# Down projection of a decoder layer on one Trainium2 core: 12 of 22 contraction blocks by a seven-product scheme

## The chip, the core and the metric

The kernel runs on one core of a Trainium2 chip. TensorE (PE, with its weight loads PEld), VectorE (DVE), ScalarE (ACT) and GpSimd (POOL) each work through a stream of instructions of their own, in order; SyncE (SP) issues most of the DMAs. The metric is the device time in microseconds of one execution, lower is better. Differences are judged on the median of several runs.

## The reference

One hybrid decoder layer is computed for 512 prompt tokens and 8 x 8 sample tokens, with model width 1024. Attention and a gated delta rule come first. The change concerns the end, the feed-forward part:

```
xn = rmsnorm(x, p['ln_ffn_pre'])
up, gate = jnp.split(xn @ p['w_ffn_in'], 2, axis=-1)
gate, new_ffn_conv = causal_dwconv(gate, ffn_conv_buf, p['ffn_conv_w'], p['ffn_conv_b'])
x = x + rmsnorm((jax.nn.gelu(gate) * up) @ p['w_down'], p['ln_ffn_post'])
```

`w_down` has 2816 rows (22 blocks of 128, the contraction) and 1024 columns (8 blocks of 128). 576 tokens go through it, 512 of the prompt and 64 samples. All of it is float32.

## The kernel before

**Products.** A float32 operand is split into a high part, a copy rounded to the type fp32r (ACT, line 314), and a low part, what the rounding lost (DVE, line 315). A product is three matmuls: high by high, high by low, low by high. The weight block of 128 x 128 is the stationary operand and the tokens stream as columns; the output stands transposed, 128 output features by tokens, in a bank of PSUM.

**Input projection.** `ffn_in` computes up and gate for each of the 22 blocks with a seven-product scheme already, on token halves of 290 columns, with weight sums on POOL. For block m, `times` (line 1895) multiplies gelu of the convolved gate by up into a buffer `gf`, once for each token half; `p7` and `p4` make the last two products of a block. `store` inside `ffn_in` transposes the conv's tails, four blocks at a time, for an output. At its end the splits of the first seven blocks begin (`divide_gf`, line 2051).

**Down projection.** `ffn_out` (line 2064) splits the other blocks: `ghi[k]` and `glo[k]` hold block k with 576 tokens. For each of 8 row blocks m of the output it takes two banks, one for tokens 256 to 575 (320 columns) and one for tokens 0 to 255, and goes through the 22 contraction blocks in chunks of 8, 8 and 6 (`chunks`). `weight` loads up to four blocks at a time (`wraw`, 256 KB) and splits them (`whi`, `wlo`). `product` makes 3 matmuls for each block. `store` (line 2098) copies the bank to `yT`, transposes it in pieces of 128 tokens, takes the sum of squares on ACT and multiplies by the norm's weight `lnfp` on DVE into `yn`. Row block 7 goes one half after the other, and `finish` (line 2129) makes the inverse roots, scales, adds the residual `x2` and stores the output.

**Order.** The program is written as straight Python loops; a list scheduler then orders each engine's stream by dependence and by the rotating buffers that a pool gives out for each name (`bufs`). `keep_in_program_order` pins single instructions. PSUM's banks have the names d (2), t (3), g (2), s (1) and m (1).

Of the kernel before, what the change touches and what calls it, by code (L numbers as in the profile page):

```python
# [9 lines left out]
F32 = mybir.dt.float32  # L10
F32R = mybir.dt.float32r
# [6 lines left out]
D = 1024  # L18
# [123 lines left out]
NC = 290  # L142
PLAIN = 3
# [7 lines left out]
class Body:  # L151
# [1618 lines left out]
    def ffn_in(self, firsts, sf, gx):  # L1770
# [6 lines left out]
        gfs = [  # L1777
            self.t(self.gtpool, [128, NQ], "gt", bufs=18) if m < 18 else None
            for m in range(NF)
        ]  # L1780
# [92 lines left out]
        def conv(st):  # L1873
# [4 lines left out]
            if i == 0:  # L1878
                self.tails = self.t(pool, [128, 18 * TAILS], "ftail", bufs=1)[:, : 18 * n]
# [15 lines left out]
        def times(eng, st, half, u):  # L1895
            if gfs[st["m"]] is None:
                gfs[st["m"]] = self.t(gx, [128, 2 * NC], f"gf{st['m']}")
            gf, y_ = gfs[st["m"]], st["y"]
            sl = slice(256 * half, 256 * half + 256)
            eng.tensor_tensor(out=gf[:, sl], in0=y_[:, sl], in1=u[:, 34:NC], op=ALU.mult)  # L1900
            eng.tensor_tensor(
                out=gf[:, 512 + 32 * half : 544 + 32 * half].rearrange("p (b t) -> p b t", b=4),
                in0=y_[:, 512:592].rearrange("p (b j) -> p b j", j=10)[:, 4 * half : 4 * half + 4, 2:10],
                in1=u[:, 0:32].rearrange("p (b t) -> p b t", b=4),
                op=ALU.mult,
            )
# [10 lines left out]
        def store():  # L1917

            if not waiting:
                return  # L1920
            m, n, tails = waiting.pop()
            tp = self.ps("s")
            self.transpose(tp[: 18 * n, :128], tails)
            rows = self.t(pool, [18 * TAILS, 128], "ftailT", bufs=1)
            nc.scalar.copy(rows[: 18 * n], tp[: 18 * n, :128])
            sl = slice(128 * m, 128 * (m + n))
            nc.gpsimd.dma_start(
                o["new_ffn_conv_prompt"][0, 0, :, sl].rearrange("r (m c) -> r m c", c=128), rows[0 : 2 * n]
            )
            nc.gpsimd.dma_start(  # L1930
                o["new_ffn_conv_sample"][0, :, :, sl].rearrange("b j (m c) -> (b j) m c", c=128), rows[2 * n : 18 * n]
            )
# [80 lines left out]
        for m in range(PLAIN, NF):  # L2013
# [22 lines left out]
            last = st  # L2036
        p7(last)
        self.gf, self.gx, self.ghi, self.glo, self.room = gfs, gx, [], [], []
        for p, j in (("hi", 1), ("lo", 1), ("hi", 2), ("lo", 2)):
            self.make_room(p, j)  # L2040
        for m in range(7):
            self.divide_gf(m)
        p4(last)
        store()

    def make_room(self, p, j):

        t = self.block_t(p, j).rearrange("p k c -> p (k c)")
        self.room += [t[:, 2 * NC * e : 2 * NC * e + SEQ + NS] for e in range(2)]

    def divide_gf(self, m, hi=None):

        hi = self.room.pop(0) if hi is None else hi
        if m == 0:
            lo = self.room.pop(0)
        elif m <= 18:
            lo = self.t(self.gtpool, [128, NQ], "gt", F32R, bufs=18)[:, : SEQ + NS]
        else:
            lo = self.t(self.gx, [128, 2 * NC], f"gf{m - 1}", F32R)[:, : SEQ + NS]
        self.split(hi, lo, self.gf[m][:, : SEQ + NS])  # L2060
        self.ghi.append(hi)
        self.glo.append(lo)

    def ffn_out(self, gh, pool, w3):
        nc, a, o = self.nc, self.a, self.o
        for m in range(7, 14):
            self.divide_gf(m, self.t(gh, [128, SEQ + NS], f"gh{m}", F32R))
        for p, j in (("hi", 3), ("lo", 3), ("hi", 4), ("lo", 4)):
            self.make_room(p, j)
        for m in range(14, NF):  # L2070
            self.divide_gf(m)
        ghi, glo = self.ghi, self.glo
        lnb = self.t(pool, [128, D], "lnfp")
        nc.scalar.dma_start(lnb, a["ln_ffn_post"][0].partition_broadcast(128))
        tiles = ((0, 128), (128, 128), (256, 128), (384, 128), (512, 64))
        groups = ((2, 5), (0, 2))
        yn = self.t(pool, [128, 5, D], "yn")
        ss = self.t(pool, [128, 5, 8], "yss")
        nc.vector.memset(ss, 1.0)
        junk = self.t(pool, [128, 128], "yjunk")  # L2080
        s1 = self.t(pool, [128, 5], "ys1")
        r = self.t(pool, [128, 5], "yr")
        roots = [self.t(pool, [128, 5], f"yroot{j}") for j in range(3)]
        nc.scalar.activation(roots[1], ss[:, :, 0], AF.Sqrt)
        x2s = []
        for i, (c0, n) in enumerate(tiles):
            x2 = self.t(pool, [128, D], "x2", bufs=5)
            nc.sync.dma_start(x2[:n], self.x2d[c0 : c0 + n])
            x2s.append(x2)

        def product(ps, w, k0, c):
            for k, (hi, lo) in enumerate(zip(*w), k0):
                gh, gl = ghi[k][:, c[0] : c[1]], glo[k][:, c[0] : c[1]]
                self.mm(ps, hi, gh, start=k == 0, stop=False)
                self.mm(ps, hi, gl, start=False, stop=False)
                self.mm(ps, lo, gh, start=False, stop=k == NF - 1)

        def store(ps, m, c, tl, late=None):
            yT = self.t(pool, [128, 320], "yT", bufs=3)
            nt = c[1] - c[0]  # L2100
            if m == 7 and tl[0] == 0:
                nc.vector.tensor_copy(yT[:, : nt // 2], ps[:, : nt // 2])
                nc.scalar.copy(yT[:, nt // 2 : nt], ps[:, nt // 2 :])
            else:
                nc.scalar.copy(yT[:, :nt], ps)
            ms = slice(128 * m, 128 * m + 128)
            if late is not None:
                for i in range(*tl):
                    t0 = tiles[i][0]
                    tp = self.ps("t")[:, :128]  # L2110
                    self.transpose(tp, yT[:, t0 - c[0] : t0 - c[0] + 128])
                    nc.scalar.activation(junk, tp, AF.Square, accum_out=ss[:, i, m : m + 1])
                    late.append((yn[:, i, ms], tp, lnb[:, ms]))
                return
            tp = self.ps4("t")
            for j, i in enumerate(range(*tl)):
                t0, n = tiles[i]
                self.transpose(tp[:n, j], yT[:, t0 - c[0] : t0 - c[0] + n])
            for j, i in enumerate(range(*tl)):
                n = tiles[i][1]  # L2120
                nc.scalar.activation(junk[:n], tp[:n, j], AF.Square, accum_out=ss[:n, i, m : m + 1])
            runs = ((0, 2, 128),) if tl[0] == 0 else ((0, 2, 128), (2, 1, 64))
            for j, nj, n in runs:
                nc.vector.tensor_tensor(
                    out=yn[:n, tl[0] + j : tl[0] + j + nj, ms], in0=tp[:n, j : j + nj],
                    in1=lnb[:n, ms].unsqueeze(1).to_broadcast([n, nj, 128]), op=ALU.mult,
                )

        def finish(tl, late):
            t = slice(*tl)  # L2130
            nc.vector.tensor_reduce(s1[:, t], ss[:, t], axis=AX.X, op=ALU.add)
            self.inverse_root(r[:, t], s1[:, t], 1.0 / D, EPS, [e[:, t] for e in roots])
            for out, tp, w in late:
                nc.vector.tensor_tensor(out=out, in0=tp, in1=w, op=ALU.mult)
            for i in range(*tl):
                c0, n = tiles[i]
                dst = o["y_prompt"][0, c0 : c0 + 128] if i < 4 else o["y_sample"].rearrange("b t d -> (b t) d")
                step = D if tl[0] else D // 2
                for d in range(0, D, step):
                    ds = slice(d, d + step)  # L2140
                    nc.vector.scalar_tensor_tensor(
                        out=yn[:n, i, ds], in0=yn[:n, i, ds], scalar=r[:n, i : i + 1], in1=x2s[i][:n, ds],
                        op0=ALU.mult, op1=ALU.add,
                    )
                    (nc.sync if (i + d // step) % 2 else nc.scalar).dma_start(dst[:, ds], yn[:n, i, ds])

        chunks = ((0, 8), (8, 8), (16, 6))
        ws = []
        for m in range(7):
            pp = [self.psd()[:, : c[1] - c[0]] for c in HALF_F]  # L2150
            for k0, nk in chunks:
                w = self.weight(a["w_down"][0], 128 * m, k0, nk)
                for p, c in zip(pp, HALF_F):
                    product(p, w, k0, c)
            if m > 3:
                ws.append(self.weight(a["w_down"][0], 128 * 7, *chunks[m - 4], pool=w3))
            for p, c, tl in zip(pp, HALF_F, groups):
                store(p, m, c, tl)
        for c, tl in zip(HALF_F, groups):
            p = self.psd()[:, : c[1] - c[0]]  # L2160
            for w, (k0, _) in zip(ws, chunks):
                product(p, w, k0, c)
            late = [] if tl[0] == 0 else None
            store(p, 7, c, tl, late)
            finish(tl, late or ())
# [43 lines left out]
```

## Time and profile before

| | |
|---|---|
| median of 3 runs | 1154.85 us (1153.15 to 1155.16) |
| profiled execution | 1153.75 us |
| its span | 1152.0 us, mean granted clock 0.996 |
| PE busy | 1115.3 us, 97% of the span |
| PEld, DVE, ACT, POOL busy | 1004.1, 717.3, 539.0, 220.5 us |
| first and last matmul of the down projection | 994.86 and 1142.60 us |

A row of the instructions by form names line, engine, operation, output and inputs, shapes, count, busy time with the mean of one, and the idle time ahead. A table of stretches gives for each stretch of the span the sum of busy time and, for engines other than the first, what they share with it. A chain lists start, duration, engine and line of the work that ended last. Line numbers belong to the kernel that the profile is of.

### The profile page before, as it was taken

The numbers are of one execution on the slowest core, as the hardware profiler recorded it, in microseconds if no ns is written. First come the engines' busy times: TensorE is split into PE (matmuls) and PEld (weight loads), VectorE is DVE, ScalarE is ACT, GpSimd is POOL, SyncE is SP. The second block draws the span as 40 slices with busy tenths as digits, with TensorE's granted clock in tenths as the row PEclk, the third lists the DMA queues.
The fourth block names the chain that finished last, engine by engine and source line by source line (L and its number), as shares of the span: only waits on it lengthen the run. The fifth ranks groups of instructions, "written<-read, shape, count | busy, mean of one in ns | idle before, by whom it ended". The sixth has DMA issues, their size and how long they took to land.

```text
span 1152.0 us, 23616 instructions
## 1 busy us (share of the span) xinstructions
PE 1115.3 (97%) x8683; PEld 1004.1 (87%) x8683; DVE 717.3 (62%) x1875; ACT 539.0 (47%) x1308; POOL 220.5 (19%) x342
## 2 busy tenths in 40 slices
PE   6999999999999999999999999999999999999997
PEld 5887887787787787789999977899999999999996
DVE  5456666695486377474343765499889889832323
ACT  5334445464464365352332344365565656732321
POOL 2022221020120010010000003333455444200000
PEclk9999999999999999999999999999999999999999
DMA  7366335737756956823232364323333332432322
GB/s 208 81 223 188 102 104 195 255 110 251 237 159 216 290 173 209 263 74 80 55 90 69 110 187 153 95 70 102 102 87 100 93 94 73 144 97 74 102 75 83
DMA packets 184347, 157.56 MB, mean 137 GB/s; under 512 B 12570, under 2 KB 146273, under 8 KB 184231
## 3 DMA queue, kind: packets, MB, share of 16 engines
q1 hardware_dynamic: 179713, 147.53, 42.0%
q0 software_dynamic: 3264, 5.16, 1.5%
q10 hardware_dynamic: 1254, 3.35, 1.0%
q8 instruction: 69, 1.13, 0.4%
q14 instruction: 47, 0.39, 0.1%
HBM read 146.12 MB, written 9.88 MB: 135 GB/s over the span
## 4 chain that ended last, share of the span: by engine, by line
PE 73%; issue 13%; DVE 6%; ACT 3%; POOL 3%; DMA 1%; SPq 0%; DVEq 0%; POOLq 0%; ACTq 0%
PE ps_d L272 26%; PE ps_t L272 18%; PE ps_g L272 15%; PE ps_s L272 7%; PE ps_t L420 7%; ACT KT L1399 1%; PE ps_m L272 1%; DVE cy L650 1%; DMA lk<-in_da_lambda_k 1%; POOL grr L384 1%; POOL gf L384 0%; DVE wlo L315 0%; DMA page<-in_cache_v 0%; POOL hss L384 0%; DVE row L970 0%
## 5 line engine op out<-in xcount | busy, mean ns | idle before, releaser
L272 PE MATMUL ps_d<-xhi,whi 128*128 128x256 f32 (+2 forms) x704 | 217.8, 310 | 0.2 <-DVE qm L1128 0.2
L315 DVE TENSOR_TENSOR wlo<-wraw,whi 128x512 fp32r<-128x512 f32 x196 | 137.9, 720 | 122.4 <-ACT whi L314 121.6
L272 PE MATMUL ps_d<-xhi,wlo 128*128 128x256 f32 (+2 forms) x704 | 213.3, 303 | 0.7 <-DVE wlo L315 0.7
L272 PE MATMUL ps_d<-xlo,whi 128*128 128x256 f32 (+2 forms) x704 | 212.8, 303 | 0.3 <-DVE xlo L315 0.2
L314 ACT CAST whi<-wraw 128x512 fp32r<-128x512 f32 (+1 forms) x198 | 117.3, 612 | 179.1 <-PE ps_d L272 93.8
L272 PEld LDWEIGHTS ps_d<-xhi,whi 128*128 128x128 f32 x704 | 133.6, 190 | 5.8 <-issue 4.2
L272 PEld LDWEIGHTS ps_d<-xlo,whi 128*128 128x128 f32 x704 | 133.9, 190 | 3.3 <-issue 2.4
L272 PEld LDWEIGHTS ps_d<-xhi,wlo 128*128 128x128 f32 x704 | 133.6, 190 | 2.5 <-issue 1.0
L1399 ACT COPY KT<-ps_t 128x512 f32<-128x512 f32 x106 | 57.2, 603 | 31.3 <-PE ps_t L420 30.8
L420 PE MATMUL ps_t<-consts,page 128*128 128x128 f32 x512 | 67.8, 279 | 0.3
L272 PE MATMUL ps_t<-fhit,hw 128*128 128x290 f32 x228 | 68.0, 298 | 0.0
L272 PE MATMUL ps_t<-flot,hw 128*128 128x290 f32 x228 | 67.7, 297 | 0.0
L272 PE MATMUL ps_t<-fhit,lw 128*128 128x290 f32 x228 | 67.6, 297 | 0.0
L420 PEld LDWEIGHTS ps_t<-consts,page 128*128 128x128 f32 x512 | 55.6, 140 | 13.8 <-issue 6.7
L314 ACT CAST hw<-sw 128x512 fp32r<-128x512 f32 x76 | 47.2, 622 | 41.4 <-PE ps_g L272 19.9
L315 DVE TENSOR_TENSOR lw<-sw,hw 128x512 fp32r<-128x512 f32 x76 | 60.1, 790 | 6.7 <-ACT hw L314 6.6
L272 PEld LDWEIGHTS ps_t<-flot,hw 128*128 128x128 f32 x228 | 43.2, 190 | 0.0
L272 PEld LDWEIGHTS ps_t<-fhit,lw 128*128 128x128 f32 x228 | 43.1, 189 | 0.0
L272 PEld LDWEIGHTS ps_t<-fhit,hw 128*128 128x128 f32 x228 | 43.0, 189 | 0.0
L1887 DVE SCALAR_TENSOR_TENSOR fy<-fpre,fw,fy 128x592 f32<-128x592 f32 x44 | 36.5, 830 | 2.5 <-ACT fy L1885 1.8
L272 PE MATMUL ps_s<-page,pT 128*32 128x256 f32 x512 | 35.3, 385 | 1.8 <-DMA page<-in_cache_v 1.6
L272 PE MATMUL ps_s<-KT,qb 128*32 128x256 f32 x512 | 35.7, 385 | 0.6
(688 smaller groups left out, 2990.1 us busy)
## 6 DMA issues: line engine op xcount, KB each, us to landing
page<-in_cache_k SPq DMA_DIRECT2D x128, 256.0 KB, 4.2
page<-in_cache_v SPq DMA_DIRECT2D x128, 256.0 KB, 4.4
wraw<-in_w_in SPq DMA_DIRECT2D x88, 256.0 KB, 3.0
wraw<-in_w_ffn_in SPq DMA_DIRECT2D x50, 256.0 KB, 3.0
wraw<-in_w_down SPq DMA_DIRECT2D x40, 256.0 KB, 3.2
raw<-in_w_ffn_in SPq DMA_DIRECT2D x38, 256.0 KB, 2.9
wraw<-in_w_out SPq DMA_DIRECT2D x16, 256.0 KB, 2.9
x<-in_x_prompt SPq DMA_DIRECT2D x4, 512.0 KB, 8.7
```

The lines of the kernel that those rows point to most:

```text
L272: return self.nc.tensor.matmul(out, lhsT, rhs, **kw).ins
L314: self.nc.scalar.copy(hi, raw)
L315: (eng or self.nc.vector).tensor_tensor(out=lo, in0=raw, in1=hi.bitcast(F32), op=ALU.subtract)
L384: nc.gpsimd.tensor_tensor(out=dst, in0=dst, in1=self.mhalf[:rows, :n], op=ALU.pow)
L420: self.nc.tensor.transpose(out, in_, self.ident[:k, :k])
L650: nc.vector.scalar_tensor_tensor(out=y, in0=pre[:, j : j + n], scalar=self.cw[:, ch, 24 + j : 25 + j], in1=y, op0=ALU.mult, op1=ALU.add)
L1399: copy(kt[:, :, 128 * j : 128 * j + 128], tp)
L1887: nc.vector.scalar_tensor_tensor(out=y, in0=pre[:, j : j + 592], scalar=fw[:, m, 16 + j : 17 + j], in1=y, op0=ALU.mult, op1=ALU.add)
```

## The change

Blocks 0 to 11 of the contraction are taken as 6 pairs (j, j + 6), the 8 row blocks as 4 pairs (2p, 2p + 1), and the 576 tokens as two halves of 288 (256 prompt tokens and 32 samples each). On each such 2 x 2 arrangement the eight block products are replaced by seven, of sums of weight blocks and of token blocks. Blocks 12 to 21 (`FLAT`: 6 and 4) stay plain, in the same halves of 288.

Pass one makes, for all four p, the three products that use unsummed token blocks (`"11"`, `"21"`, `"22"`), in two steps of three pairs (`stage_s`), and keeps sums in `saves`; `stage_l` adds the plain blocks of the upper row block there, ahead of them for p of 0 and 1 and after them for 2 and 3. Pass two takes p in turn: the plain blocks of the lower row block (`stage_f`), then t1 and t2 (`stage_t`), then t3 and t4 (`stage_e`). Weight loads of the seven products fetch three blocks with 256 columns (384 KB, `dx`, six buffers, two for each step). The token sums of t1 to t4 are made late in pass one by `sums_seven`, on ACT, DVE and POOL. Each of the 30 or so stages loads two stages ahead and prepares one ahead. The tail of the kernel scales on ACT and adds on POOL for one tile and a half, and the rest goes as before.

```
+NH = 288
+JS = 6
+STEPS = ((0, 3), (3, 3))
+FLAT = ((12, 6), (18, 4))
...
+        self.leads = self.weight(a["w_down"][0], 0, *FLAT[0])
         p7(last)
...
+        for m in range(2 * JS, 18):
+            self.divide_flat(m)
         p4(last)
-        store()
+        self.last_tail = store
...
+    def divide_seven(self, j, gh):
...
+        self.split(ab[:, 0:2], ab[:, 2:4], x)
+        self.split(c[:, 0], c[:, 1], y[:, 1])
+        g.tensor_tensor(out=y[:, 0], in0=y[:, 0], in1=x[:, 1], op=ALU.subtract)
+        g.tensor_tensor(out=y[:, 1], in0=y[:, 1], in1=y[:, 0], op=ALU.subtract)
...
+    def sums_seven(self, j):
...
+        self.pinned_split(c, lo, y)
+        t2 = y[:, 1].unsqueeze(1).to_broadcast([128, 2, NH])
+        self.nc.gpsimd.tensor_tensor(out=y, in0=t2, in1=ab[:, 0:2].bitcast(F32), op=ALU.subtract)
+        yield
+        self.tc.keep_in_program_order(
+            self.nc.vector.tensor_tensor(out=y, in0=y, in1=ab[:, 2:4].bitcast(F32), op=ALU.subtract)
+        )
+        yield
+        self.pinned_split(ab[:, 0:2], ab[:, 2:4], y)
...
+        def both(p, k0, nk):
+            t = self.t(w7, [128, 768], "dx", bufs=6).rearrange("p (k c) -> p k c", k=3)
+            nc.sync.dma_start(t, w[128 * k0 : 128 * (k0 + nk), 256 * p : 256 * p + 256].rearrange("(k p) c -> p k c", p=128))
+            return t[:, :, 0:128], t[:, :, 128:256]
...
+        def stage_s(p, i, banks):
...
+            def load():
+                x, y = both(p, k0, nk), both(p, JS + k0, nk)
+                op(nc.gpsimd, x[1], x[1], y[1], ALU.add)
+                return *x, y[0]
+
+            def prepare(raws):
+                a11, a21, a12 = raws
+                op(nc.vector, a21, a11, a21)
+                ws = [pair(a11), pair(a12)]
+                op(nc.vector, a21, a12, a21, ALU.add)
+                return [*ws, pair(a21)]
+
+            def run(ws):
+                b1, b2, b3 = banks()
+                product(b1, ws[0], "11", start=first, stop=end, **kw)
+                product(b2, ws[1], "21", start=first and p > 1, stop=end and p < 2, **kw)
+                product(b3, ws[2], "22", start=first and p > 1, stop=end and p < 2, **kw)
...
+        def finish(h, late=()):
...
+            nc.vector.tensor_copy(r4[32 * h : 32 * h + 32], r[last, 3 * h + 2 : 3 * h + 3])
...
+                    if i == 3 or i == 4 and d == 0:
+                        nc.scalar.activation(
+                            yn[rows, i, ds], yn[rows, i, ds], AF.Identity, scale=r[:, i + h : i + h + 1] if i < 4 else r4
+                        )
+                        op(nc.gpsimd, yn[rows, i, ds], yn[rows, i, ds], x2s[i, d][rows], ALU.add)
+                        nc.sync.dma_start(dst[:, ds], yn[rows, i, ds])
+                        continue
...
+        for i in range(len(stages) + 2):
+            if i < len(stages):
+                loaded.append(stages[i][0]())
+            if 0 < i <= len(stages):
+                ready.append(stages[i - 1][1](loaded.pop(0)))
+            if i > 1:
+                at[0] = i - 2
+                stages[i - 2][2](ready.pop(0))
```

The instructions of DVE move at three places (on PE, fourteen matmuls of 288 columns of the first plain stage stand ahead of the last up product where seven of 320 stood). On DVE, at the end of the splits, ahead of the first weights that follow the first plain stage (`wlo_13440` now; `gt`, `fhit`, `flot`, `ghab` name low parts of token blocks). Before:

```order
L315 TENSOR_TENSOR gt_13339<-gt_9910,flot_2491_13327 128x576
L315 TENSOR_TENSOR gt_13342<-gf_2396_12830,fhit_2492_13328 128x576
L315 TENSOR_TENSOR wlo_13501<-wraw_13496,whi_13500 128x512
L315 TENSOR_TENSOR gf_2499_13345<-gf_2426_12985,fhit_2492_13328 128x576
L315 TENSOR_TENSOR wlo_13504<-wraw_13498,whi_13500 128x256
L315 TENSOR_TENSOR gf_2500_13348<-gf_2455_13139,flot_2493_13329 128x576
L315 TENSOR_TENSOR gf_2501_13351<-gf_2463_13239,flot_2493_13329 128x576
```

and now:

```order
L319 TENSOR_TENSOR gt_13336<-gt_9908,gt_13336 128x288
L319 TENSOR_TENSOR gt_13344<-gt_9909,gt_13344 128x288
L319 TENSOR_TENSOR ghab_2493_13351<-gt_9904,ghab_2493_13351 128x576
L319 TENSOR_TENSOR gt_13352<-gt_9910,gt_13352 128x288
L2151 MEMSET yss_13368 128x48
L319 TENSOR_TENSOR wlo_13440<-wraw_13383,whi_13439 128x512
L319 TENSOR_TENSOR gf_2496_13360<-gf_2468_13250,gt_13359 128x576
L2190 TENSOR_TENSOR dx_13482<-dx_13482 128x3x128
L319 TENSOR_TENSOR lw_13522<-dx_13482,hw_13521 128x384
```

Of the splits of token blocks the last of the seven-product ones are 576 and 288 columns in turn, the next low weight part comes behind them, and the first subtraction of weight blocks (`dx`) behind that.

On DVE in the middle of the projection: `wlo` is a low part of plain weights, `yn` the output that is weighted by `lnfp`, `dx` raw weights of a step of `stage_s` or their sums, `lw` low parts of them, `yT` an output on its way to a transpose. Before:

```order
L2124 TENSOR_TENSOR yn_13356<-ps_t_14103,lnfp_13354 128x2x128
L2124 TENSOR_TENSOR yn_13356<-ps_t_14103,lnfp_13354 64x128
L2124 TENSOR_TENSOR yn_13356<-ps_t_14114,lnfp_13354 128x2x128
L315 TENSOR_TENSOR wlo_14292<-wraw_14287,whi_14291 128x512
L315 TENSOR_TENSOR wlo_14245<-wraw_14240,whi_14244 128x512
L315 TENSOR_TENSOR wlo_14248<-wraw_14242,whi_14244 128x256
```

and now, where steps of `stage_s` follow each other in pass one:

```order
L2190 TENSOR_TENSOR dx_13704<-dx_13704 128x3x128
L2190 TENSOR_TENSOR dx_13704<-dx_13706,dx_13704 128x3x128
L2190 TENSOR_TENSOR yT_13702<-ps_d_13393,consts_13377 128x288
L319 TENSOR_TENSOR lw_13711<-dx_13654,hw_13710 128x384
L319 TENSOR_TENSOR lw_13715<-dx_13656,hw_13714 128x384
L319 TENSOR_TENSOR lw_13720<-dx_13654,hw_13719 128x384
L2190 TENSOR_TENSOR dx_13754<-dx_13754 128x3x128
L2190 TENSOR_TENSOR dx_13754<-dx_13756,dx_13754 128x3x128
L2190 TENSOR_TENSOR yT_13752<-ps_g_13444,consts_13377 128x288
L319 TENSOR_TENSOR lw_13761<-dx_13704,hw_13760 128x384
L319 TENSOR_TENSOR lw_13765<-dx_13706,hw_13764 128x384
```


The two sums of a step's weights stand ahead of the low parts of the step before it; before, low parts of weights stood there with nothing but the products by `lnfp`.

On DVE at the end of the kernel, before:

```order
L2102 COPY yT_14870<-ps_d_14803 128x128
L2134 TENSOR_TENSOR yn_13356<-ps_t_14873,lnfp_13354 128x128
L2131 TENSOR_REDUCE ys_2506_13360<-yss_13357 128x2
L2134 TENSOR_TENSOR yn_13356<-ps_t_14876,lnfp_13354 128x128
L394 TENSOR_SCALAR yroot_2508_13362<-ys_2506_13360 128x2
L396 TENSOR_SCALAR yroot_2510_13364<-ys_2506_13360 128x2
L397 RECIPROCAL yr_13361<-yroot_2509_13363 128x2
L398 TENSOR_TENSOR yroot_2509_13363<-yr_13361 128x2
L399 TENSOR_TENSOR yroot_2509_13363<-yroot_2509_13363,yroot_2510_13364 128x2
L400 SCALAR_TENSOR_TENSOR yr_13361<-yroot_2509_13363,yr_13361 128x2
L2141 SCALAR_TENSOR_TENSOR yn_13356<-yn_13356,yr_13361,x_2511_13366 128x512 x2
L2141 SCALAR_TENSOR_TENSOR yn_13356<-yn_13356,yr_13361,x_2512_13368 128x512 x2
```

and now:

```order
L2190 TENSOR_TENSOR yT_15132<-ps_d_14885,fw_13363 128x288
L2245 TENSOR_REDUCE ys_2501_13370<-yss_13368 128x3
L2249 TENSOR_TENSOR yn_13367<-ps_t_15134,lnfp_13365 128x2x128
L398 TENSOR_SCALAR yroot_2504_13373<-ys_2501_13370 128x3
L400 TENSOR_SCALAR yroot_2506_13375<-ys_2501_13370 128x3
L2249 TENSOR_TENSOR yn_13367<-ps_t_15134,lnfp_13365 32x128
L401 RECIPROCAL yr_13371<-yroot_2505_13374 128x3
L402 TENSOR_TENSOR yroot_2505_13374<-yr_13371 128x3
L403 TENSOR_TENSOR yroot_2505_13374<-yroot_2505_13374,yroot_2506_13375 128x3
L404 SCALAR_TENSOR_TENSOR yr_13371<-yroot_2505_13374,yr_13371 128x3
L2247 COPY yr_2503_13372<-yr_13371 32x1
L2262 SCALAR_TENSOR_TENSOR yn_13367<-yn_13367,yr_13371,dx_15004 128x512
```

The eviction is an addition of 288 columns, a product by `lnfp` and a copy of a scale stand between the sum of squares and the scalings, and five scalings of 512 columns follow (the first shown) where four stood.

## What the change will do: the prediction

> **What bounds the kernel now.** I read the page's busy times first, then the table of stretches over the last 200 us, the chain that ended last, and the instructions by form. The busy times name the candidate, and the stretches show that it holds in the stage that the change rewrites.
>
> ```profile
> PE 1115.3 (97%) x8683; PEld 1004.1 (87%) x8683; DVE 717.3 (62%) x1875; ACT 539.0 (47%) x1308; POOL 220.5 (19%) x342
> 950.00:1000.00 50.00, 50.00 (x371) 49.94 (x371) 45.01 (x82) 34.77 (x65) 19.87 (x32) 1.00 0.31 94
> 1000.00:1050.00 50.00, 50.00 (x381) 49.66 (x380) 20.74 (x35) 18.21 (x50) 0.57 (x1) 1.00 0.38 110
> 1050.00:1100.00 50.00, 49.21 (x372) 48.58 (x372) 15.16 (x29) 17.14 (x55) 0.00 (x0) 1.00 0.33 94
> 1100.00:1143.00 43.00, 42.87 (x324) 42.16 (x322) 12.07 (x27) 10.80 (x40) 0.00 (x0) 1.00 0.15 48
> ```
>
> The columns are PE, PEld, DVE, ACT and POOL, then clock and DMA. From about 1000 us on, the down projection keeps PE busy without a gap at full clock, while DVE and ACT need a third of the time and POOL nothing. A matmul saved there is worth its cadence as long as the others can take on more work. Matmul records overlap, so I take cadences from the chain, where runs of equal matmuls stand end to end.
>
> ```profile
> 994.86 0.54 PE L272 MATMUL ps_t<-fhit,whi 128*128 128x320 f32 x2
> 988.49 3.23 PE ps_t L272 x24
> 1003.06 3.52 PE ps_t L272 x24
> 1006.58 2.84 PE ps_d L272 x24
> 1071.18 16.62 PE ps_d L272 x126
> 1089.37 16.62 PE ps_g L272 x126
> 1142.60 0.28 PE L272 MATMUL ps_d<-flot,wlo 128*128 128x256 f32 x1
> ```
>
> 24 matmuls of 290 columns take 3.23 us (134.6 ns each), of 320 columns 3.52 (146.7), of 256 columns 2.84 (118.3). Cost follows columns. One row block of the output is 66 of each width, 17.5 us; the two 126-rows start 18.19 apart, so five transposes take 0.7 us, 0.14 each.
>
> **Matmuls.** Before: 8 row blocks x 22 contraction blocks x 3 = 528 at each width: 528 x 146.7 + 528 x 118.3 = 139.9 us. After: 10 plain blocks give 8 x 10 x 3 x 2 = 480, and the seven products of 6 block pairs and 4 output pairs give 4 x 6 x 7 x 3 = 504: 984 of 288 columns. Between the 256 and 320 rows 288 comes to 132.5 ns; a 290 that is not reduced at all would be 134.6. I take 133, nearer the first since columns set the cost: 130.9 us. **Gain 9.0**, bounds 9.5 and 7.5.
>
> **Transposes.** A store now transposes 288 tokens in three full pieces, 16 stores x 3 = 48 against 40. Ahead of the last matmul stand 45 against 38: 7 x 0.14 = **+1.0**.
>
> **Waits of PE that go.** From 994.86 to 1142.72 PE spends 147.9 us: 139.9 of down matmuls, 1.6 of twelve late up matmuls, 39 transposes at 0.14 (5.6, the conv tails' one among them). **0.7** is left as waiting; it goes with the code that caused it.
>
> **The hand-over.** These rows price the splits and the queue of DVE.
>
> ```profile
> 999.27 0.41 DVE L1900 TENSOR_TENSOR gf<-fy,ps_t 128x256 f32<-128x256 f32 x1
> 999.70 3.94 DVE L315 TENSOR_TENSOR gt<-gt,gh 128x576 fp32r<-128x576 f32 x5
> L315 DVE TENSOR_TENSOR gt<-gt,gh 128x576 fp32r<-128x576 f32 x7 | 5.3, 758 | 0.1
> L315 DVE TENSOR_TENSOR lw<-sw,hw 128x512 fp32r<-128x512 f32 x76 | 60.1, 790 | 6.7 <-ACT hw L314 6.6
> L315 DVE TENSOR_TENSOR wlo<-wraw,whi 128x256 fp32r<-128x256 f32 x8 | 3.4, 420 | 0.9 <-ACT whi L314 0.9
> L315 DVE TENSOR_TENSOR wlo<-wraw,whi x34: 418/692/694, 1011.0 to 1098.2; 128x512 fp32r<-128x512 f32 x29, 128x256 fp32r<-128x256 f32 x5
> ```
>
> PE starts on blocks 12 to 17, ready early, with 14 matmuls ahead of the last up product where seven stood, so that product ends about 0.9 us later, covered. Behind it come 22 + 36 matmuls, 7.7 us from 998.4: PE wants the next weights' low part at 1006.2. On DVE that part stands behind seven splits of 576 and five of 288 from about 999.5: at 0.67 to 0.79 each for the long ones (0.758 less overlap, or the five in 3.94) and 0.4 for the short ones 6.9 to 7.7 us, and its own 0.6. It comes at 1006.9 to 1007.8, **+0.7** (0.6 to 1.6). No earlier: POOL's second differences wait for those splits, behind them POOL's first weight sum. The six first 384 KB loads start when the last up product frees their space, 1.0 us for issue, and have until 1012.6, PE's start S on the seven-product blocks.
>
> **Pass one is the doubtful place.** A stage there is 27 matmuls, 3.6 us. DVE does five 384-wide operations for it, 0.56 each by the straight line from the 0.42 and 0.69 rows: 2.8 us; ACT three copies; POOL one addition. Each fits. What need not fit is a ring: six load buffers hold three stages, and DVE runs in order.
>
> ```profile
> L1805 POOL TENSOR_TENSOR sw<-raw,raw 128x512 f32<-128x512 f32 x19 | 24.9, 1312 | 25.7 <-DVE lw L315 24.5 <-DMA raw<-in_w_ffn_in 1.2
> wraw<-in_w_down SPq DMA_DIRECT2D x40, 256.0 KB, 3.2
> page<-in_cache_k SPq DMA_DIRECT2D x128, 256.0 KB, 4.2
> x<-in_x_prompt SPq DMA_DIRECT2D x4, 512.0 KB, 8.7
> L310 SPq DMA_DIRECT2D wraw<-in_w_down x34: 367/368/460, 1011.7 to 1098.9; - x34
> L1910 DVE TENSOR_TENSOR p<-ps_t,p 128x290 f32<-128x290 f32 x19 | 8.6, 454 | 0.0
> ```
>
> The third low part of stage n frees its buffers; SP issues both loads for stage n+3 (2 x 0.37), they land (3.9, between the 3.2 of a quiet queue and the 4.2 of a full one), POOL adds (1.0, three quarters of 1.3), DVE forms two sums (1.1) and evicts a bank (0.45), and only then comes the first low part of stage n+2 (0.5): 8.0 us with 0.3 for semaphores, 9.0 with the other two low parts, for two stages, in which PE spends 7.2. The lead at the start pays for most of it. Stage 2's third low part stands at S + 2.3 (its buffer is released at S + 1.2, and DVE has three plain weights ahead of it). By the same ring stage 4 gets its first at S + 10.6, wanted at 11.0; stage 6 at S + 19.6, wanted at 18.2. The other chain, stages 3, 5, 7 (S + 6.5, 14.5, 23.5), just meets PE. **+1.5**, from 0 (landing in 3.2) to 5 (landing in 5). Plain weight loads stand in SP's queue between these; each can delay them by 0.37 and is counted once.
>
> GPSIMD Engine Reference, section of the specifications, in the Trainium skill, says that GpSimd and VectorE share SBUF interfaces and contend when a VectorE operation has two SBUF inputs, which speaks against adding GpSimd work here. The rows agree as far as they go: 790 ns for a 512-wide split in the stage where POOL works, 692 in the one where it idles. By that ratio a stage's DVE work is 3.2 us and the ring 0.2 longer: PE still bounds, and it would add about 0.3 to the sum.
>
> After pass one come 120 plain matmuls, 16 us, under which six blocks are summed and split anew (18 DVE operations of 576, 12 to 14 us, beside 5 of weights): full, but the second half is wanted only 10 us later. In pass two PE needs 17.6 us for each output pair and DVE some 11.5, so I add nothing; without that cover a wait is 0.5 us in each of four pairs.
>
> **The tail.**
>
> ```profile
> 1142.92 0.29 DVE L2102 COPY yT<-ps_d 128x128 f32<-128x128 f32 x1 [0.17 <-PE ps_d L272]
> 1143.69 0.28 ACT L2112 ACTIVATE yjunk<-ps_t 128x128 f32<-128x128 f32 x1
> 1144.11 0.28 ACT L2112 ACTIVATE yjunk<-ps_t 128x128 f32<-128x128 f32 x1
> 1144.51 0.17 DVE L2131 TENSOR_REDUCE ys<-yss 128x2 f32<-128x16 f32 x1
> 1146.01 2.74 DVE L2141 SCALAR_TENSOR_TENSOR yn<-yn,yr,x 128x512 f32<-128x512 f32 x4
> L2124 DVE TENSOR_TENSOR yn<-ps_t,lnfp 128x256 f32<-128x256 f32 x15 | 6.2, 414 | 20.1 <-ACT yjunk L2121 20.1
> wraw<-in_w_down SPq DMA_DIRECT2D x8, 128.0 KB, 2.2
> ```
>
> From the last matmul's start to the end 9.4 us pass. Now the eviction is one 288-wide sum (0.45 for 0.29: +0.15), DVE may still be at the other half's scaling (+0.3), there are three squares (+0.45), a 256-wide product stands between the sum of squares and the root (+0.35), a copy of a scale (+0.15), and a fifth scaling (+0.7): **+2.1**. If the last store, 128 KB, lands a microsecond sooner than one of 256 KB, +1.1; if nothing overlaps, +3.
>
> **Sum.** -9.0 + 1.0 - 0.7 + 0.7 + 1.5 + 2.1 = -4.4 us. The profiled execution took 1153.75 us (span 1152.0 and 1.75 around it), 1.1 below the median of the runs: it becomes 1149.4, and the median of 1154.85 becomes **1150.4**. With every bound good but the loads' 3.2: -9.5 + 1.0 - 0.7 + 0.6 + 0 + 1.1 = -7.5. What a measurement here can tell from no change is 0.2%, 2.3 us.
>
> **Rivals.** *Full cover* (chance 0.13): the loads land in 3.2 us and the last store early: -7.5, 1147.4. For it: wraw's row, DMA engines busy 0.31 to 0.38. Against it: two 384 KB loads go out together.
>
> *The ring eats the gain* (0.18): loads land in about 5 us, stages 4, 6 and 8 each come 2 us later than the last, waits of 5 to 6: 1154 to 1155. For it: the page loads' 4.2 with less in flight per load; the 0.7 of the hand-over may be 1.6 as well.
>
> *Slower* (0.27): the same ring with landings near the 8.7 of the first x loads, as when lnfp, x2, plain weights and six loads are in flight together. The ring is then 13.8 us for two stages, 6.9 for one against 3.6; over the five stages that use a second-hand buffer 16 us, less 2 of lead: +14 instead of +1.5, 1163. It turns the sign where waits pass 6.6 us, a landing of about 5.4. Against it: only four loads in the trace are so slow, at the start of the program.
>
> TensorE: Matmul & The Clock Gate, Part 1, in the Trainium skill, says that an idle window of some 3.4 us halves the matmul clock until a busy one has passed; the trace has 1.00 in every stretch of the projection and no wait that long there. By it a stall of 3.5 us or more would cost about another 1.7 us; single waits of the ring are 1.4 to 2, so the sum and the forecast hold without it.
>
> *It does not do what it says*: not possible for the count, since the matmuls are written out; 984 is fixed.
>
> **Chances.** Forecast 0.42 (own range 1148 to 1152.4), full cover 0.13: faster 0.55. The ring eating the gain 0.18: same. Slower 0.27. The range reaches from 1146.5, below full cover, to 1160, which takes in the lower half of the slower case; some 0.17 is left out.
>
> **What would show it.** Right: 984 matmuls of 288 columns at 132 to 134 ns; PE gaps, 1 to 2 us each, ahead of the first product of the sixth stage of pass one and ahead of the third plain stage; the tail 11 to 12 us. Wrong: a cadence above 135; gaps in every stage of pass one; gaps in pass two; loads that land in over 5 us.

## The result, and the profile after

The changed kernel takes 1175.33 us (median of 6 runs, 1173.78 to 1176.98) where the kernel before takes 1154.00 (1151.23 to 1155.79): ratio 1.0181, 95% interval 1.0167 to 1.0195. The forecast was 1150.4, so it lies 25 us off and on the wrong side.

The page of the changed kernel and its table of stretches (PE, PEld, DVE, ACT, POOL, clock, DMA), to set beside those of before:

```profile
PE 1113.3 (95%) x8619; PEld 1000.2 (85%) x8619; DVE 795.0 (68%) x1981; ACT 557.8 (48%) x1363; POOL 289.7 (25%) x396
1000.00:1050.00 50.00, 45.44 (x323) 44.11 (x322) 42.23 (x71) 27.94 (x61) 24.13 (x22) 0.97 0.67 204
1050.00:1100.00 50.00, 43.73 (x308) 42.85 (x307) 36.28 (x51) 18.23 (x44) 19.15 (x14) 0.93 0.28 84
1100.00:1150.00 50.00, 46.50 (x351) 45.59 (x351) 32.15 (x66) 25.61 (x86) 15.20 (x13) 1.00 0.21 67
1150.00:1173.00 23.00, 8.05 (x61) 7.58 (x59) 12.61 (x33) 6.20 (x23) 4.67 (x3) 0.75 0.29 103
```

PE, almost without a gap before, now loses 3.5 to 6.3 us in each 50, the clock falls below 1, and DVE, a third busy before, is busy for 64 to 84%. PE's waits from 760 us on (us in total, times, longest) say where:

```profile
PE ps_t L2229 <- DVE yT L2190: 5.4, 5, 2.2
PE ps_g L276 <- ACT whi L318: 4.0, 1, 4.0
PE ps_d L276 <- DVE wlo L319: 3.0, 1, 3.0
PE ps_t L2229 <- DVE yn L2241: 2.9, 2, 1.5
PE ps_t L276 <- ACT u L1850: 2.5, 1, 2.5
PE ps_g L276 <- DVE wlo L319: 1.1, 1, 1.1
```

Nearly all of it is DVE that comes late (ACT's `whi` too: its cast stood in ACT's stream behind a token sum that DVE had not made). The wait of 3.0 us is the hand-over, the passage from the input projection to the down projection. DVE and POOL there, in order of time (start, duration):

```profile
1005.43 0.74 DVE L319 TENSOR_TENSOR fhit<-gt,fhit 128x576 fp32r<-128x576 f32 x1
1006.10 1.36 DVE L319 TENSOR_TENSOR flot<-gt,flot 128x576 fp32r<-128x576 f32 x1
1007.39 0.45 DVE L319 TENSOR_TENSOR gt<-gt,gt 128x288 fp32r<-128x288 f32 x1
1007.76 0.75 DVE L319 TENSOR_TENSOR ghab<-gt,ghab 128x576 fp32r<-128x576 f32 x1
1008.42 2.25 DVE L319 TENSOR_TENSOR gt<-gt,gt 128x288 fp32r<-128x288 f32 x2
1010.60 1.34 DVE L319 TENSOR_TENSOR ghab<-gt,ghab 128x576 fp32r<-128x576 f32 x1
1012.89 0.63 DVE L319 TENSOR_TENSOR wlo<-wraw,whi 128x512 fp32r<-128x512 f32 x1
...
1005.59 1.26 POOL L2084 TENSOR_TENSOR gt<-gt 128x288 f32<-128x288 f32 x1 [1.73 <-DVE gt L319]
1007.92 1.25 POOL L2084 TENSOR_TENSOR gt<-gt 128x288 f32<-128x288 f32 x1
1009.25 1.12 POOL L2190 TENSOR_TENSOR dx<-dx,dx 128x384 f32<-128x384 f32 x1
1010.32 2.27 POOL L2084 TENSOR_TENSOR gt<-gt 128x288 f32<-128x288 f32 x2
```

The same subtraction of 576 columns takes 0.74 and 0.75 us where it starts just ahead of a subtraction on POOL, and 1.36 and 1.34 where one of POOL's is already running; two of 288 take 2.25 where 0.9 would do. DVE's operations with an input in PSUM do not show this: 288-wide additions from a bank are at 0.44 to 0.46 everywhere, beside POOL or not.

The tail, DVE first, then the SP queue and POOL:

```profile
1157.35 1.77 DVE L2262 SCALAR_TENSOR_TENSOR yn<-yn,yr,gt 128x512 f32<-128x512 f32 x1
1159.15 0.46 DVE L2190 TENSOR_TENSOR yT<-ps_d,fw 128x288 f32<-128x288 f32 x1
...
1163.58 3.75 DVE L2262 SCALAR_TENSOR_TENSOR yn<-yn,yr,dx 128x512 f32<-128x512 f32 x4
1167.25 0.73 DVE L2262 SCALAR_TENSOR_TENSOR yn<-yn,yr,x 64x512 f32<-64x512 f32 x1
...
1166.14 0.50 SPq L2260 DMA_DIRECT2D out_y_sample<-yn  x1
1166.74 1.02 SPq L2266 DMA_DIRECT2D out_y_prompt<-yn  x2
...
1164.38 1.73 POOL L2190 TENSOR_TENSOR yn<-yn,x 64x512 f32<-64x512 f32 x1 [4.14 <-ACT yn L2256]
```

The last product's eviction (`yT`) stands behind a scaling that took 1.77 us beside POOL's addition; four scalings take 3.75 us where 2.74 stood before; and in SP's queue two stores of finished rows stand behind the sample's, which waits for POOL.

Three marks of each profiled execution show where a kernel's time lies: the first matmul of the down projection, its last one, and the end.

| kernel | first | last | projection, last minus first | tail, end minus last | median, us |
|---|---|---|---|---|---|
| before | 994.86 | 1142.60 | 147.7 | 9.4 | 1154.00 |
| changed | 998.74 | 1157.21 | 158.5 | 16.0 | 1175.33 |
| all sums on DVE (e1) | 993.49 | 1135.16 | 141.7 | 16.0 | 1154.21 |
| weight and late token sums on DVE (e2) | 1001.22 | 1143.54 | 142.3 | 16.0 | 1159.25 |
| token differences on DVE (e3) | 996.78 | 1155.49 | 158.7 | 16.0 | 1173.14 |
| tail order alone (e4) | 996.51 | 1154.20 | 157.7 | 15.1 | 1174.18 |
| e1 with the tail reordered (e6) | 992.00 | 1133.32 | 141.3 | 12.3 | 1150.55 |
| e6 with early weights (e7) | 997.08 | 1137.76 | 140.7 | 12.2 | 1151.22 |
| e1 with idle additions on POOL (e8) | 998.49 | 1167.21 | 168.7 | 16.4 | 1182.45 |

The first mark also moves between executions, with the attention stages far ahead of the change: it stands at 994.86 in the kernel before and at 999.06 in the same kernel with idle work on POOL (e5, below), whose edit comes behind it. The projection (147.7 and 147.9) and the tail (9.4 and 9.5) do not move there.

Between the first two marks PE waits 14.3 us in the changed kernel and 3.6 with all sums on DVE. In the changed kernel the clock is also at half for some 10 us behind two of these waits (3.4 at the hand-over; 0.54 on average from 1065.5 to 1072.6). That is 10.7 and, by estimate, 5 of the 16.8 us between the two projections.

### The profile page after: what moved, and what is told of

The parts are those of the page before. It is cut to its first block, busy times and chain, and to the rows that moved or that the text cites. A ratio compares the mean times of both kernels' runs of the same rounds, so it can differ in the third digit from the quotient of the medians.

```text
span 1173.2 us, 23848 instructions
## 1 busy us (share of the span) xinstructions
PE 1113.3 (95%) x8619; PEld 1000.2 (85%) x8619; DVE 795.0 (68%) x1981; ACT 557.8 (48%) x1363; POOL 289.7 (25%) x396
## 4 chain that ended last, share of the span: by engine, by line
PE 64%; issue 15%; DVE 9%; POOL 4%; ACT 4%; DMA 3%; SPq 0%; DVEq 0%; POOLq 0%; ACTq 0%
PE ps_d L276 23%; PE ps_g L276 13%; PE ps_t L276 13%; PE ps_t L424 7%; PE ps_s L276 6%; ACT KT L1403 1%; POOL dx L2190 1%; DVE lw L319 1%; PE ps_m L276 1%; DMA dz<-in_w_down 1%; DMA dx<-in_w_down 1%; DVE wlo L319 1%; POOL grr L388 1%; DVE gt L319 1%; DVE yn L2262 1%
## 5 line engine op out<-in xcount | busy, mean ns | idle before, releaser
L319 DVE TENSOR_TENSOR wlo<-wraw,whi 128x512 fp32r<-128x512 f32 x172 | 130.4, 774 | 59.9 <-ACT whi L318 59.4
L318 ACT CAST whi<-wraw 128x512 fp32r<-128x512 f32 (+1 forms) x174 | 103.6, 611 | 119.8 <-PE ps_d L276 77.9
L276 PE MATMUL ps_t<-fhit,hw 128*128 128x290 f32 (+1 forms) x244 | 71.5, 298 | 2.5 <-ACT u L1850 2.5
L319 DVE TENSOR_TENSOR lw<-sw,hw 128x512 fp32r<-128x512 f32 x76 | 68.9, 906 | 5.2 <-ACT hw L318 5.2
L276 PE MATMUL ps_t<-flot,hw 128*128 128x290 f32 (+1 forms) x248 | 72.4, 297 | 0.0
L276 PE MATMUL ps_t<-fhit,lw 128*128 128x290 f32 (+1 forms) x236 | 70.2, 298 | 0.1
L318 ACT CAST hw<-sw 128x512 fp32r<-128x512 f32 x76 | 46.7, 617 | 14.3 <-PE ps_g L276 12.5
L276 PEld LDWEIGHTS ps_t<-flot,hw 128*128 128x128 f32 x248 | 46.5, 190 | 0.0
L318 ACT CAST hw<-dx 128x384 fp32r<-128x384 f32 x48 | 24.1, 513 | 42.0 <-POOL dx L2190 24.3
L1901 ACT ACTIVATE fy<-fpre,fw 128x592 f32<-128x592 f32 x22 | 19.5, 885 | 50.2 <-DVE fpre L1861 50.0
L319 DVE TENSOR_TENSOR lw<-dx,hw 128x384 fp32r<-128x384 f32 x48 | 36.8, 791 | 9.5 <-ACT hw L318 9.4
```

What stands on the lines that cost most here:

```text
L276: return self.nc.tensor.matmul(out, lhsT, rhs, **kw).ins
L318: self.nc.scalar.copy(hi, raw)
L319: (eng or self.nc.vector).tensor_tensor(out=lo, in0=raw, in1=hi.bitcast(F32), op=ALU.subtract)
L1901: nc.scalar.activation(y, pre[:, 0:592], AF.Identity, bias=fw[:, m, 19:20], scale=fw[:, m, 16:17])
```

## The experiments

Two theories stood against each other after the result, and a third was left from the prediction. *Exclusion*: a DVE operation with both inputs in SBUF is drawn out while POOL runs one of its own. *Load*: DVE has too much to do, whoever else works. *Ring*: the six weight buffers and their landing set pass one.

**Who makes the sums.** In the first kernel all of them go to DVE.

```
-        g = self.nc.gpsimd
+        g = self.nc.vector
...
-        self.nc.gpsimd.tensor_tensor(out=y, in0=t2, in1=ab[:, 0:2].bitcast(F32), op=ALU.subtract)
+        self.nc.vector.tensor_tensor(out=y, in0=t2, in1=ab[:, 0:2].bitcast(F32), op=ALU.subtract)
...
-                op(nc.gpsimd, x[1], x[1], y[1], ALU.add)
+                op(nc.vector, x[1], x[1], y[1], ALU.add)
...
-                op(nc.gpsimd, a21, a21, a22, ALU.add)
-                op(nc.gpsimd, a11, a21, a11)
+                op(nc.vector, a21, a21, a22, ALU.add)
+                op(nc.vector, a11, a21, a11)
...
-                op(nc.gpsimd, a21, a22, a11)
+                op(nc.vector, a21, a22, a11)
```

> All 48 or so additions and subtractions that the changed down projection gives to POOL (token differences, token sums, weight sums of both passes) go to DVE; the tail keeps its POOL work. Exclusion theory (a DVE operation with both inputs in SBUF is drawn out while POOL runs one of its own, 0.95 against 0.54 us at 384 columns, and POOL's 1.0 to 1.9 us stand in the chains): DVE's operations fall back to 0.55, 0.69 and 0.75 us, the waits of 3.0 us at the hand-over and 5.1 us in the middle shrink to under 2 each, their slow clock goes, 1158 to 1166 us. Load theory (DVE simply has too much to do, whoever else works): some 22 us more of DVE work, 1178 to 1190. Ring theory (the six weight buffers and their landing set the pace): 1172 to 1177.

Measured: 1154.21 us (10 runs, 1150.78 to 1155.77), ratio to before 0.9988 (0.9968 to 1.0007). All 21 us are gone, more than the theory asked for; Load and Ring both fall. PE's waits, from 760 us on:

```profile
PE ps_t L2229 <- DVE yT L2190: 3.0, 2, 2.2
PE ps_d L276 <- DVE wlo L319: 2.1, 2, 1.3
PE ps_t L2229 <- DVE yn L2241: 0.5, 1, 0.5
```

DVE does more here than in the changed kernel and is not busier for it: 790.5 us against 795.0. What it gained in operations it saved on those drawn out.

The second kernel leaves out the first line of that diff (the token differences), the third has that line alone.

> Only the weight sums of both passes and the late token sums go from POOL to DVE; the token differences at the hand-over stay on POOL. Exclusion: the hand-over keeps its wait of 3.0 us and the 2.5 us wait in the input projection, the middle and the four output pairs lose most of theirs, 1164 to 1169. Load: 1177 to 1187. Ring: 1173 to 1177.

Measured: 1159.25 us (10 runs, 1156.76 to 1162.61), ratio 1.0031 (1.0015 to 1.0047). The hand-over's wait stays (2.38 us), as does that in the input projection (2.33); middle and output pairs keep 0.3 to 0.4 us at a time. It gains 16 us where 6 to 11 were expected. Its projection is only 0.6 us longer than the first experiment's, so most of the 5 us that it lacks lie ahead of it.

> Only the twelve token differences of the seven-product blocks go from POOL to DVE. Exclusion: the 2.5 us wait of the input projection (a weight sum queued on POOL behind two of these differences) goes, and the hand-over's 3.0 us with 1.5 us of slow clock falls to under 1.5: 1168 to 1172. Load: DVE is busy 47.8 of 50 us in the input projection, twelve more operations of 0.4 us there and at the hand-over make waits: 1177 to 1182. If the hand-over is bound by the number of splits alone: 1174 to 1177.

Measured: 1173.14 us (4 runs, 1172.3 to 1173.26), ratio 1.0145 (1.0113 to 1.0177). The half on the input projection holds: no wait of PE is left there. The half on the hand-over misses: its wait is 2.86 us. POOL's weight sums still run beside DVE there, and five of the differences now stand in DVE's own queue. A new wait of 2.1 us stands in pass one. The two parts' gains, 16 and 2, make 18 of the 21 (by the ratios to before, 17 and 4 of 22).

In the changed kernel's input projection the wait of 2.5 us comes about on POOL. Its rows there:

```profile
784.92 2.99 POOL L2083 TENSOR_TENSOR gt<-gt,gt 128x288 f32<-128x288 f32 x1 [5.97 <-DVE gt L1915]
787.87 1.74 POOL L1821 TENSOR_TENSOR sw<-wraw,raw 128x512 f32<-128x512 f32 x1
```

One token difference of a finished block (not two, as the expectation has it) stands ahead of a sum of weights (`sw`). It takes 2.99 us there, the same width at the hand-over 1.1 to 1.3, so POOL is held up beside DVE as well. The sum starts at 787.87; before, the same sum started at 781.61. Of these 6.3 us the execution has 2.7, by which it is later already at 750 us. The loads that wait for its buffers, and ACT's casts of them, move with it.

**Exclusion shown on the kernel before.** POOL, idle in the down projection, gets work that nobody reads (e5).

```
+        def beside(m, yT, nt):
+            for _ in range(6):
+                if m % 2:
+                    nc.gpsimd.tensor_copy(pj[:, :nt], yT[:, :nt])
+                else:
+                    nc.gpsimd.tensor_tensor(out=pj[:, :nt], in0=yT[:, :nt], in1=x2s[0][:, :nt], op=ALU.add)
```

> The kernel before, with idle POOL given work that nobody uses during the down projection: for each half of an even row block six additions of two SBUF inputs (320 or 256 columns), of an odd one six copies of one input. Exclusion: DVE's 512-wide low parts beside the additions take 1.0 us and more where 0.69 stood, beside the copies less or nothing, its operations with an input in PSUM stay at 0.41; PE stays fed, since DVE has two thirds of its time free there: within 2 us of before. If POOL's additions in the changed kernel were not what drew DVE's operations out: all at 0.69.

Measured: 1155.63 us (10 runs, 1151.8 to 1159.77), ratio 1.0009 (0.9993 to 1.0024). POOL and DVE there:

```profile
1035.07 6.68 POOL L2103 COPY pj<-yT 128x320 f32<-128x320 f32 x12 [6.45 <-ACT yT L2114]
1053.32 11.50 POOL L2105 TENSOR_TENSOR pj<-yT,x 128x320 f32<-128x320 f32 x12 [11.56 <-ACT yT L2114]
...
1037.17 0.96 DVE L315 TENSOR_TENSOR wlo<-wraw,whi 128x512 fp32r<-128x512 f32 x1 [3.50 <-ACT whi L314]
1038.48 0.69 DVE L315 TENSOR_TENSOR wlo<-wraw,whi 128x512 fp32r<-128x512 f32 x1 [0.35 <-ACT whi L314]
1039.09 0.94 DVE L2135 TENSOR_TENSOR yn<-ps_t,lnfp 128x256 f32<-128x256 f32 x3
1050.55 1.29 DVE L315 TENSOR_TENSOR wlo<-wraw,whi 128x512 fp32r<-128x512 f32 x2 [5.32 <-ACT whi L314]
1055.35 2.56 DVE L315 TENSOR_TENSOR wlo<-wraw,whi 128x512 fp32r<-128x512 f32 x2 [3.50 <-ACT whi L314]
1057.83 0.94 DVE L2135 TENSOR_TENSOR yn<-ps_t,lnfp 128x256 f32<-128x256 f32 x3
```

Two low parts take 1.29 us with POOL idle and 2.56 beside its additions: double. One beside copies takes 0.69 to 0.96. The three operations with an input in PSUM take 0.94 beside either.

Single records show that the order decides. The low part of 0.96 started 0.04 us behind a copy. The one of 0.69, at 1038.48, started 0.03 us ahead of a copy, and that copy took 0.92 us where copies beside nobody take 0.40 to 0.46. So a copy on POOL holds DVE up and is held up as an addition is; it is only shorter than one (an addition alone takes 0.73 to 0.87).

The time does not move, because DVE has room there: drawn-out operations cost nothing until DVE is the one waited for.

**Exclusion or POOL's own slowness?** An addition of 384 columns takes POOL 1.0 us and more, and the changed kernel puts it in chains where DVE needs 0.55. The first experiment takes both away. The next keeps all sums on DVE and has POOL work beside for nobody.

```
+        def beside(e, f):
+            f = f.rearrange("p k c -> p (k c)").bitcast(F32)
+            for _ in range(2):
+                nc.gpsimd.tensor_tensor(out=x4[e % 2][64:128, 0:384], in0=f[64:128], in1=lnb[64:128, 0:384], op=ALU.add)
...
                 ws = [pair(a11), pair(a12)]
+                beside(0, ws[0][0])
```

> All sums on DVE, and 56 additions of 384 columns on POOL beside the splits of weights, whose results nobody reads: about as much POOL work as the changed kernel has there, but none of it in a chain. Exclusion alone (DVE's operations drawn out are the price): the lw splits go from 0.55 to 0.8 on average again and a good half of the 21 us comes back, 1162 to 1172. If the price was POOL's own time in the chains (1.0 to 1.9 us for an addition where DVE takes 0.55): 1154 to 1156.

Measured: 1182.45 us (4 runs, 1182.06 to 1185.35), ratio 1.0254 (1.0237 to 1.0271), 28 us more than the first experiment and 10 more than exclusion was expected to give. DVE is busy for 823.6 us where it was 790.5 with the same work of its own. Among the waits of this run none is for one of these additions, on any engine: they cost only what they do to DVE. The same splits in the three kernels, the changed one, all sums on DVE, and this one (minimum, median, maximum in ns), and the additions:

```profile
L319 DVE TENSOR_TENSOR lw<-dx,hw x48: 543/554/1785, 1016.0 to 1145.9; 128x384 fp32r<-128x384 f32 x48
```

```profile
L319 DVE TENSOR_TENSOR lw<-dx,hw x48: 544/549/560, 1009.6 to 1122.6; 128x384 fp32r<-128x384 f32 x48
```

```profile
L319 DVE TENSOR_TENSOR lw<-dx,hw x48: 544/560/1380, 1016.6 to 1157.2; 128x384 fp32r<-128x384 f32 x48
L2163 POOL TENSOR_TENSOR x<-hw,lnfp 64x384 f32<-64x384 f32 x56 | 70.4, 1269 | 80.0 <-ACT hw L318 77.9
```

With POOL silent the spread is 16 ns. So exclusion alone is enough for a loss of this size; POOL's slowness is not needed for it. The loss passes the 21 us of the changed kernel, but POOL works more here, 70.4 us in these additions against some 56 in the changed kernel's sums from the hand-over to the last matmul. What POOL's slowness adds in the changed kernel, where its results are waited for, was not taken apart.

**The tail.** In the first of these kernels only the order on DVE changes: eviction of the last product, then the two scalings of the finished half.

```
-                    finish(1)
+                    roots_of(1)
+                    scale(1, (3,))
...
-                    store(out(b4, u), 2 * p + 1, 0, late)
-                    finish(0, late)
+                    pin(nc.vector.tensor_tensor(out=t, in0=b4, in1=u, op=ALU.add))
+                    store(t, 2 * p + 1, 0, late)
+                    scale(1, (2,))
+                    roots_of(0, late)
+                    scale(0, (0, 1, 4))
```

> The eviction of the last product is put ahead of the two scalings of the finished half on DVE; nothing else changes. If the order on DVE makes PE's last wait of 2.16 us, that wait falls to about 0.5 and the end comes 1.2 to 1.8 us sooner: 1173.5 to 1174.1. If the scalings then delay the inverse roots by as much, or the output's DMAs set the end, no change: 1175 to 1176.

Measured: 1174.18 us (4 runs, 1171.05 to 1176.27), ratio to before 1.0163 (1.0127 to 1.0198). PE's wait falls from 2.16 to 0.55 us, the tail from 16.0 to 15.1; the gain of 1.2 us in the median is too small for these runs to be sure of. The second joins it with the sums on DVE, puts one of the two scalings ahead of the eviction, the sample's scalings on DVE as the last, and the third tile's stores on SP.

> All sums on DVE as in the first experiment, and the tail reordered: one scaling of the finished half, then the eviction of the last product, then the second scaling; the sample tile's two scalings on DVE, behind the others; the stores of the third tile issued by SP. If PE's last wait of 2.16 us and the order of DVE's work and of SP's queue (two 256 KB stores behind one that waits for POOL) make the longer tail: last matmul to end 16 us to 12 to 13, 1150 to 1152. If the volume of stores at the end sets it (1.28 MB against 1.05): 15 us, 1153 to 1154.

Measured: 1150.55 us (12 runs, 1147.31 to 1156.02), ratio 0.9974 (0.9961 to 0.9988): 0.26% under the kernel before, by little but clear of the noise. The tail is 12.3 us. Its rows:

```profile
1132.79 0.75 DVE L2264 SCALAR_TENSOR_TENSOR yn<-yn,yr,gf 128x512 f32<-128x512 f32 x1
1133.65 0.46 DVE L2445 TENSOR_TENSOR yT<-ps_d,fw 128x288 f32<-128x288 f32 x1
1134.03 1.22 DVE L2264 SCALAR_TENSOR_TENSOR yn<-yn,yr,gt 128x512 f32<-128x512 f32 x1
...
1138.08 2.74 DVE L2264 SCALAR_TENSOR_TENSOR yn<-yn,yr,dx 128x512 f32<-128x512 f32 x4
1140.74 1.40 DVE L2264 SCALAR_TENSOR_TENSOR yn<-yn,yr,x 64x512 f32<-64x512 f32 x2
```

Four scalings are back at 2.74. Which of the three steps gave how much of the 3.7 us was not taken apart.

**The hand-over's order.** As that kernel, with the split of the second plain stage's weights written ahead of the splits of the seven-product blocks.

```
             if 0 < i <= len(stages):
                 ready.append(stages[i - 1][1](loaded.pop(0)))
+            if i == 2:
+                late_splits()
```

> As the kernel with all sums on DVE and the tail reordered, and the first two plain stages' weights are prepared ahead of the splits of the seven-product blocks. If the hand-over's wait of 1.3 us is only a matter of that order: 1 to 1.5 us less than that kernel. If DVE is then late for the first seven-product stage instead: no gain, the wait stands some 6 us later.

Measured: 1151.22 us (12 runs, 1149.68 to 1153.91), ratio 0.9970 (0.9961 to 0.9980). No gain: a wait of 1.35 us stands at the same place, 13 us behind the first mark, as the 1.42 of the kernel without this edit. The edit missed what PE waits for. PE has run both first stages (36 matmuls each) by then and waits for the low part of the third stage's weights. In both kernels the second stage's low parts are made some 5 us ahead of the first mark (987.07 and 992.15), and the third's stands behind the splits on DVE (1005.63 and 1010.57). So whether this order makes the wait stays untested.

## Why the prediction was wrong, point by point

**The step that failed** is the price of POOL's work. The prediction weighed it by one ratio of means, 790 ns for a split where POOL works against 692 where it doesn't, put it at "about 0.3" and left even that out of the sum. The trace of before had the two populations inside that mean; the view of one tile's instructions gives minimum, median and maximum:

```profile
L315 DVE TENSOR_TENSOR lw<-sw,hw x76: 679/693/1781, 752.2 to 982.6; 128x512 fp32r<-128x512 f32 x76
```

Half of the 76 take 693 ns or less, and the worst 1781: an operation that meets POOL is not 14% slower, it is up to 2.6 times as long. Single records have 17 of the 76 at 1.05 to 1.78 us, and each of these started while one of POOL's sums of weights was running. At the mean's excess of 0.1 us the 46 operations that POOL gets from the hand-over to the end would cost DVE 5 us, at the worst's, 1.1 us, 51. The range had room for the first and not for the second, on an engine that the prediction itself had at 2.8 of 3.6 us a stage. On the `lw` splits alone it came to 48 x (0.791 - 0.550), 11.6 us, by their means in the changed kernel and with all sums on DVE. The slower case that was given a chance of 0.27 came, by another mechanism than the one named.

SBUF — State Buffer, section "Who interferes with whom", in the Trainium skill, says that a VectorE instruction with two SBUF inputs contends with a GpSimd instruction that reads SBUF, and that the one that starts second is blocked for the whole of the other. The rows agree in who is hit (two SBUF inputs: 1.29 to 2.56; one input in PSUM: 0.94 and 0.94), and they agree in the full block. Two rows of the changed kernel:

```profile
1060.10 1.88 POOL L2108 TENSOR_TENSOR gt<-gt,fhit 128x576 f32<-128x576 f32 x1 [1.37 <-DVE gt L2093]
1060.61 1.78 DVE L319 TENSOR_TENSOR lw<-dx,hw 128x384 fp32r<-128x384 f32 x1
```

POOL's operation has 1.37 us left when DVE's starts, and DVE's ends 0.41 behind it. Of the 21 `lw` splits of this kernel that start while POOL's operation runs, 20 take what is left of it and about 0.42 more, 0.62 to 1.79 us in all; the five that overlap POOL but started first take 0.55.

- *Matmuls, -9.0*: right. 18 of 288 columns take 2.38 us in the changed kernel's chain, 132.4 ns each: 130.3 us, a gain of 9.6.
- *Transposes, +1.0, and old waits, -0.7*: with the sums on DVE the projection is 6.1 us shorter (141.7 against 147.7). Its waits come to 1.31 + 0.52 + 0.77 + 0.12 + 0.83 = 3.6, and 147.7 - 9.6 + 1.0 - 0.7 + 3.6 = 142.0.
- *Hand-over, +0.7 (0.6 to 1.6)*: 3.0 in the changed kernel, and about 1.5 of slow clock behind it (below). With the sums on DVE 1.31: the queue was counted rightly, the durations weren't.
- *Ring in pass one, +1.5*: the one longer wait there, 1.5 us ahead of transposes, is for a `yn` product queued behind drawn-out splits, none is for a load; with the sums on DVE 0.5 is left. The two rivals that went by this ring did not come about: the loads of 384 KB landed in 3.2 us in the median. With the sums on DVE they landed in 6.1, above the 5.4 at which the ring was to turn the sign, and still no wait of PE was for one.
- *Pass two, 0*: four pairs with waits of 0.5 to 1.4, 4.6 us together; with the sums on DVE 0.95. Middle of the projection, also 0: 4.0 and 1.1 us, where DVE makes the late token sums (18 operations, seen and called "full, but") and POOL's six subtractions of 1.7 to 1.9 us run among them; behind the 4.0 the clock fell to half as well.
- *Tail, +2.1 (1.1 to 3)*: 6.6. The eviction behind the scaling was put at 0.3, and PE waited 2.16 for it (0.39 before); the rest is drawn-out scalings and SP's queue. Put in order it is 2.9.
- *Input projection*: no term. The change moves nothing there that the prediction looked at, but six of its token differences are ready block by block and run there: a wait of 2.5 us.

With sums off POOL and the tail in order the kernel measures 1150.55, what was forecast; that is the sum's other terms coming together (-6.4 for the projection, +2.9 for the tail) in another kernel, not the forecast being right.

## What to carry to other kernels

Ahead of giving an idle engine work, ask whether it holds up the busy one, and look in the trace of before at minimum, median and maximum of one tile's operations, not at a mean: they show two populations at once. Price a meeting by what is left of the other engine's operation when it is met. Work given to POOL here cost DVE as much as if DVE had done it itself (795.0 us busy without it, 790.5 with it). Where DVE must share time with POOL, operations with an input in PSUM are the ones that aren't hit (0.44 to 0.46 us beside POOL or not).

## What the runs showed of the hardware

Waits of PE of 2 to 3 us halved its clock, and not always. The changed kernel after the hand-over's 2.99 us (stretches: PE, PEld, DVE, ACT, POOL, clock):

```profile
1013.50:1014.80 1.30, 1.22 (x8) 1.09 (x8) 1.30 (x3) 1.23 (x3) 1.30 (x2) 1.00 0.12 37
1014.80:1018.20 3.40, 3.40 (x15) 3.35 (x15) 3.40 (x4) 0.01 (x1) 2.14 (x2) 0.50 0.51 148
1018.20:1021.00 2.80, 2.80 (x22) 2.70 (x22) 2.80 (x7) 2.25 (x5) 0.00 (x0) 0.99 0.46 131
```

15 matmuls in 3.4 us of which 26 would have fitted: some 1.5 us for a wait of 3. The loss begins 1.3 us after PE is back and lasts 3.4; at the same place in e3 it began 0.9 us before PE was back and lasted 6.8. After waits of 2.33 and 2.38 us (e2) and 2.13 (e3) the clock fell to 0.50 as well; after the wait of 2.48 us in the changed kernel's input projection it stayed at 1.00:

```profile
791.00:794.30 3.30, 0.85 (x7) 0.61 (x5) 0.81 (x2) 1.46 (x4) 0.00 (x1) 1.00 0.80 231
794.30:797.00 2.70, 2.67 (x20) 2.67 (x20) 2.56 (x6) 1.45 (x3) 0.83 (x2) 1.00 0.00 0
```

After waits of 1.5 us and less that stand alone, the clock stayed at 1.00 in all ten profiled runs from 740 us on. The prediction took single waits under 3.5 us to be free of this; here one of 2 to 3 us can cost half as much again, by where it falls.

TensorE: Matmul & The Clock Gate, Part 1, in the Trainium skill, calls the window of 3.4 us free-running, which would make it a matter of phase, of where in that window the wait falls. The runs fit that, but waits well under the window's 3.4 us were enough, and there the measurement decides. One wait of 1.92 us stands near 750 us in every profiled run, ahead of the work that the change adds: the clock fell to 0.50 behind it in four of them (the kernel before, e2, e5 and e8) and stayed at 1.00 in the other six. The wait near 790 us was followed by 0.50 in e2 (2.33 us) and not in the changed kernel (2.48) or e4 (2.40), which have the same code up to there. What sets the moment no run shows. The trace of before already had such a fall behind a wait under 3.5 us, so it could have been seen ahead of the prediction.
